# Up projections of a two-layer trunk on one core: three couples of groups instead of two, and two convolution taps multiplied on ScalarE

## The chip, the cores and the metric

The kernel runs on one core of a Trainium2 chip. The metric is the device time of one execution in microseconds; of several runs the median is given. The engines are TensorE (PE, with its weight load PEld), VectorE (DVE), ScalarE (ACT), GpSimd (POOL) and SyncE (SP); transfers go through queues of SP and of POOL.

## The reference, cut to what matters

Two layers of a token mixer and a gated MLP on 256 tokens of width 2048, all in float32. The change lies in the up projection, the convolution and the gate of the MLP:

```python
def conv_ffn(x, w_up, conv_w, conv_b, w_down):
    h = x @ w_up                       # (256, 2048) @ (2048, 11008)
    C = h.shape[-1]
    h = lax.conv_general_dilated(h, conv_w[:, None, :], window_strides=(1,),
                                 padding=[(CONV_W - 1, 0)],
                                 dimension_numbers=('NWC', 'WIO', 'NWC'),
                                 feature_group_count=C) + conv_b
    a, g = jnp.split(h, 2, axis=-1)
    return (jax.nn.silu(g) * a) @ w_down
```

The convolution is causal with three taps: a channel's value at token t is the sum of three tokens t, t-1, t-2, each times a constant of the channel.

## The kernel before, in words

**Products.** Each float32 operand is split into a rounded high part and the low rest, and a product is built of high x high, high x low and low x high. A weight chunk is 128 x 2048 values. It is loaded by SP's queue (`_load`, L105 and L109, three raw rooms), cast to `wh` by ScalarE (L134), and the rest `wl` is subtracted by VectorE (L137). All matmuls stand in line L242.

**Groups.** An up projection has 22 groups, numbered 0 to 21, of four chunks (the last one has two); group 0 is computed at the boundary ahead of it. A group yields two blocks of 128 channels of `a` and two of `g`. There are two ways to compute groups:

- `plain(gi, turned)`: channels on the partitions, tokens along the row. `prod_a` makes 64 matmuls of 512 columns (with `wh`) and 64 of 256 (with `wl`). One accumulator then has two halves of 256 tokens, which `sum_halves` (L409 copy on ScalarE, L411 addition on VectorE) adds.
- `summed(gis)`, a couple: two groups at once, tokens on the partitions. It takes eight chunks in the order `UP_PAIRS`; four are treated as *wide* with 24 matmuls of 512 columns (`eight`), four as *seven* (`UP_SEVEN`) with 21, in the manner of Strassen's seven products. A *seven* chunk needs sums of weights (`ts`, L144) and five rooms (`ts`, `wh`, `wl`, `th`, `tl`), and a combined sum of inputs (`combine`, rooms `xu`). Its banks are named q3, p2, e, q4, p1, q5, p7, p6. At the end, `rest` (L474 to L478) and four additions (L1119) give the values, and the plain group that follows turns them back: 16 transposes into `upr` (L1049), and behind its chunks 1 and 2 it calls `both`, which works through the four pairs of the couple.

**Pair.** `pair` convolves a block of `a` and its block of `g` (`conv`: ScalarE scales by the third tap and adds the bias, L1023; VectorE adds the other taps with two scalar_tensor_tensor, L1024 and L1026), then silu on ScalarE (L1040) and the product on VectorE (L1041). A plain group ends with its two pairs, so their instructions stand in the queues of ScalarE and VectorE among the first splits of what follows.

**Order of the work.** `UP` lists groups and couples: before, 5+6 and 8+9. `EARLY` puts side work behind chunk c of group gi: `restore` (the row's layer norm gets its scale and offset: two rows of constants loaded, four operations on VectorE, L741 and L742), `combine` (one of the four combined sums, L1074 and L314 to L326) and `park` (a store of the residual on POOL's queue). `jobs` is `park_all`: for chunks of the down projection it loads, splits and stores parts ahead of time, one step for each call of `next(jobs)`. Its loads and stores are on POOL's queue.

**Rooms.** The ring `big` has 14 rooms of 128 x 2048 and holds split weights, the combined sums and most activations; `side` has 6. Small tiles of 256 columns are in ring `t1` (T1 rooms), of 512 in `t2` (T2 rooms).

The Tile scheduler orders the instructions of an engine. Each engine runs its queue in that order, so a waiting instruction holds back all that stand behind it.

Of the kernel before, what the change touches and what calls it, by code (L numbers as in the profile page):

```python
# [56 lines left out]
T1, T2 = 6, 5  # L57
# [15 lines left out]
UP = [(1,), (2,), (3,), (4,), (5, 6), (7,), (8, 9), *((i,) for i in range(10, 22))]  # L73
UP_PAIRS = [0, 2, 1, 3, 5, 4, 6, 7]
UP_SEVEN = (2, 3, 4, 6)
EARLY = {(1, 2): ("restore", 0), (2, 1): ("combine", 0), (2, 2): ("restore", 1), (2, 3): ("park", 0),
         (3, 1): ("restore", 2), (3, 2): ("combine", 1), (3, 3): ("restore", 3), (4, 0): ("park", 1),
         (4, 1): ("combine", 2), (4, 2): ("combine", 3)}
# [143 lines left out]
def trunk(ctx: ExitStack, tc: tile.TileContext, x, xT, gm_in, gm_wout, ffn_up, ffn_dn,  # L222
# [12 lines left out]
    def slot(shape, name, dt=F32, tag="big"):  # L235
        return big.tile(shape, dt, tag=tag, name=name, bufs=SLOTS[tag])
# [169 lines left out]

    def sum_halves(acc, name):
        lo = tp.tile([P, S], F32, tag="t1", name=f"lo_{name}", bufs=T1)
        nc.scalar.copy(lo, acc[:, S : 2 * S])  # L409
        h = tp.tile([P, S], F32, tag="t1", name=f"h_{name}", bufs=T1)  # L410
        nc.vector.tensor_tensor(h, acc[:, 0:S], lo, ALU.add)  # L411
        return h
# [605 lines left out]
    def conv(layer, F, acc, name):  # L1018

        h = acc if acc.shape[-1] == S else sum_halves(acc, name)  # L1020
        w = C_CONV + (layer * 2 * NF_FF + F) * 4
        c = tp.tile([P, S], F32, tag="t1", name=f"c_{name}", bufs=T1)
        nc.scalar.activation(c, h, AF.Identity, bias=cst[:, w + 3 : w + 4], scale=cst[:, w + 2 : w + 3])  # L1023
        nc.vector.scalar_tensor_tensor(c[:, 1:S], h[:, 0 : S - 1], cst[:, w + 1 : w + 2], c[:, 1:S],  # L1024
                                       ALU.mult, ALU.add)
        nc.vector.scalar_tensor_tensor(c[:, 2:S], h[:, 0 : S - 2], cst[:, w : w + 1], c[:, 2:S],  # L1026
                                       ALU.mult, ALU.add)
        return c

    def ffn(layer, ln, acc, end, last):  # L1030
# [3 lines left out]
        def pair(a, acc_a, acc_g):  # L1034
            if act[a // 8] is None:
                act[a // 8] = slot([P, 8, S], f"act{layer}_{a // 8}", tag="side" if a // 8 in (0, 5) else "big")
            ca = conv(layer, a, acc_a, f"{layer}a{a}")
            cg = conv(layer, NF_FF + a, acc_g, f"{layer}g{a}")
# [31 lines left out]
        def combine_up(p):  # L1070
# [4 lines left out]
            if len(sums) % 2 == 0:  # L1075
                rooms.append(slot([P, 2, 8 * P], f"xu{layer}_{p}", F32R))
# [4 lines left out]
        def plain(gi, turned):  # L1081
# [3 lines left out]
            for c in range(KD // nk):  # L1085
# [7 lines left out]
                if (gi > 9 and c > 0) or (gi, c) == (7, 3):  # L1093
                    next(jobs, None)
# [466 lines left out]
```

## Time and profile before

| | us |
|---|---|
| median of 3 runs | 2451.52 (2451.03 to 2452.03) |
| the profiled execution | 2450.69 |
| its span in the profile | 2448.9 |
| busy: PE / PEld | 2441.2 / 2066.0 |
| busy: DVE / ACT / POOL | 2187.1 / 1510.8 / 140.2 |

Busy times are those of one profiled execution; the span is the time from its first to its last record. Matmuls are pipelined, so TensorE can be busy without a gap and still be slower than at its peak. Up stages are at 817 to 1264 us (first layer) and 1772 to 2219 us (second layer). L with a number is a line of the kernel before; names such as `wh178` carry the chunk's number, and the profile leaves numbers out. An up_ with a letter is a bank of a couple, `up` an accumulator of a plain group.

### The profile page before, as it was taken

How to read it: one execution, taken by the hardware profiler on the slowest of the kernel's cores; microseconds unless marked ns; L12 is line 12 of the kernel's file. 1: busy time of each engine (PE TensorE's matmuls, PEld its weight loads, DVE VectorE, ACT ScalarE, POOL GpSimd, SP SyncE). 2: the span in 40 equal slices, each digit the busy share in tenths (PEclk: the TensorE clock that was granted, in tenths of full speed). 3: DMA queues.
4: the chain of work that ended last, by engine and by line, in shares of the span. 5: the costliest groups of instructions: out<-in, count | busy, mean ns of one | idle time of the engine just before them, and what ended most of it. 6: DMA issues, size and time to landing. Idle time of an engine off the chain costs nothing.

```text
span 2448.9 us, 32246 instructions
## 1 busy us (share of the span) xinstructions
PE 2441.2 (100%) x12154; PEld 2066.0 (84%) x12154; DVE 2187.1 (89%) x2909; ACT 1510.8 (62%) x1995; POOL 140.2 (6%) x261
## 2 busy tenths in 40 slices
PE   9999999999999999999999999999999999999999
PEld 7888888888888888888888888988888888888887
DVE  7999999889998889998889897878798998888998
ACT  6666665566576655666665566665665666666553
POOL 0000000001010000011000000000000001010000
PEclk9999999999999999999999999999999999999999
DMA  7555666658796655799988885543575589898894
GB/s 293 204 206 206 232 202 206 206 172 302 256 296 241 239 203 194 260 356 377 338 322 320 317 299 170 189 143 126 205 275 180 179 337 363 321 368 304 313 353 178
DMA packets 128763, 627.37 MB, mean 256 GB/s; under 512 B 11592, under 2 KB 15184, under 8 KB 91616
## 3 DMA queue, kind: packets, MB, share of 16 engines
q1 hardware_dynamic: 94224, 462.47, 53.1%
q0 software_dynamic: 34384, 162.86, 17.8%
q8 instruction: 95, 1.56, 0.2%
q14 instruction: 60, 0.49, 0.1%
HBM read 552.35 MB, written 72.93 MB: 255 GB/s over the span
## 4 chain that ended last, share of the span: by engine, by line
PE 95%; DVE 2%; issue 1%; DMA 1%; ACT 1%; SPq 0%; ACTq 0%; DVEq 0%
PE up L242 29%; PE ub L242 16%; PE dn_q L242 8%; PE dn_p L242 6%; PE v_q L242 5%; PE v_p L242 4%; PE up_q L242 2%; PE wo_q L242 2%; PE dn_e L242 2%; PE up_p L242 2%; PE wo_p L242 2%; PE upf L242 2%; PE mo L242 2%; PE v_e L242 2%; PE mkv L242 1%
## 5 line engine op out<-in xcount | busy, mean ns | idle before, releaser
L137 DVE TENSOR_TENSOR wl<-raw,wh 128x1024 fp32r<-128x1024 f32 (+5 forms) x611 | 937.7, 1553 | 106.3 <-ACT wh L134 76.3
L134 ACT CAST wh<-raw 128x1024 fp32r<-128x1024 f32 (+5 forms) x611 | 791.2, 1318 | 312.9 <-PE up L242 72.0
L242 PE MATMUL up<-xhl,wh 128*128 128x512 f32 x2112 | 492.9, 390 | 0.0
L242 PEld LDWEIGHTS up<-xhl,wh 128*128 128x128 f32 x2112 | 392.3, 188 | 78.6
L134 ACT CAST th<-ts 128x1536 fp32r<-128x1536 f32 x194 | 201.5, 1052 | 164.2 <-DVE ts L144 136.9
L242 PEld LDWEIGHTS up<-xhl,wl 128*128 128x128 f32 x2112 | 262.4, 192 | 5.1
L242 PE MATMUL up<-xhl,wl 128*128 128x256 f32 x2112 | 265.1, 283 | 0.0
L137 DVE TENSOR_TENSOR tl<-ts,th 128x1536 fp32r<-128x1536 f32 x194 | 229.6, 1223 | 9.1 <-ACT th L134 4.7
L242 PE MATMUL ub<-wh,xhl 128*128 128x512 f32 x564 | 175.7, 393 | 0.0
L144 DVE TENSOR_TENSOR ts<-ts,raw 128x512 f32<-128x512 f32 x194 | 133.9, 690 | 2.0
L242 PEld LDWEIGHTS ub<-wh,xhl 128*128 128x128 f32 x564 | 105.9, 188 | 23.7 <-issue 1.9
L144 DVE TENSOR_TENSOR ts<-raw 128x1024 f32<-128x1024 f32 x97 | 118.5, 1222 | 2.7 <-DMA raw<-in_gm_in_dram 1.0
L242 PE MATMUL ub<-wl,xhl 128*128 128x512 f32 x282 | 109.8, 389 | 0.0
L242 PE MATMUL v_q<-wh,xhl 128*128 128x512 f32 x224 | 70.7, 391 | 0.1
L242 PEld LDWEIGHTS ub<-wl,xhl 128*128 128x128 f32 x282 | 53.0, 188 | 11.1
L242 PE MATMUL v_p<-wh,xhl 128*128 128x512 f32 x192 | 59.9, 389 | 0.0
L242 PEld LDWEIGHTS v_q<-wh,xhl 128*128 128x128 f32 x224 | 42.1, 188 | 9.7 <-ACT wh L134 1.0
L832 ACT ACTIVATE lny<-lnt,lncol 128x128 f32<-128x128 f32 x96 | 36.5, 469 | 15.7 <-PE lnt L828 15.6
L161 DVE TENSOR_TENSOR praw<-praw 128x512 f32<-128x512 f32 x64 | 44.1, 690 | 0.5
L242 PE MATMUL v_q<-wl,xhl 128*128 128x512 f32 x112 | 43.6, 389 | 0.0
L242 PE MATMUL mo<-wh,oT 128*128 128x512 f32 x128 | 42.7, 411 | 0.0
L242 PEld LDWEIGHTS v_p<-wh,xhl 128*128 128x128 f32 x192 | 36.1, 188 | 7.5
(2073 smaller groups left out, 4820.9 us busy)
## 6 DMA issues: line engine op xcount, KB each, us to landing
raw<-in_ffn_up_dram SPq DMA_DIRECT2D x172, 1024.0 KB, 5.7
raw<-in_gm_in_dram SPq DMA_DIRECT2D x93, 1024.0 KB, 5.2
raw<-in_ffn_dn_dram SPq DMA_DIRECT2D x68, 1024.0 KB, 7.9
raw<-in_gm_wout_dram SPq DMA_DIRECT2D x48, 1024.0 KB, 6.5
praw<-in_ffn_dn_dram POOLq DMA_DIRECT2D x16, 1024.0 KB, 12.8
keptth<-pth POOLq DMA_DIRECT2D x16, 1024.0 KB, 8.5
kepttl<-ptl POOLq DMA_DIRECT2D x16, 1024.0 KB, 8.8
fth<-keptth POOLq DMA_DIRECT2D x16, 1024.0 KB, 9.6
```

What stands on the lines that cost most here:

```text
L134: cast = self.nc.scalar.copy(hi, raw)
L137: self.nc.vector.tensor_tensor(lo, raw, hi.bitcast(F32), ALU.subtract)
L144: add = lambda o, a, b: self.nc.vector.tensor_tensor(o, a, b, ALU.add)
L161: add = lambda o, a, b: pin(nc.vector.tensor_tensor(o, a, b, ALU.add))
L242: recent[0] = nc.tensor.matmul(o, l, r, start=start, stop=stop, skip_group_check=True)
L832: nc.scalar.activation(y[:, j], t[:, j * P : (j + 1) * P], AF.Identity, bias=lncol[:, o : o + 1], scale=lncol[:, g : g + 1])
```

## The change

- `UP` has three couples, 3+4, 6+7 and 9+10. In the first layer couple 9+10 holds chunks 180 to 187.
- `conv_both` replaces `sum_halves` and `conv` for pairs of plain groups: `a` and `g` share tiles of 2 x 256. ScalarE multiplies taps 2 and 3 as well, with `nc.scalar.mul`, four per pair, and VectorE adds both products with one addition per tap over both halves. `conv` stays for the pairs that come from the transposes.
- `EARLY`: all four combines, two restores and one park are in groups 1 and 2; the restores 2 and 3 and the second park are in groups 12, 16 and 17.
- The rooms of combined sums are taken from `side` instead of `big`.
- Parking starts at (8, 3) and is called behind every chunk of groups 13 to 15, in groups 11, 12 and 16 to 21 behind chunks 1 to 3.
- `T1`, `T2` are 5 and 6 instead of 6 and 5.

```diff
-T1, T2 = 6, 5
+T1, T2 = 5, 6
...
-UP = [(1,), (2,), (3,), (4,), (5, 6), (7,), (8, 9), *((i,) for i in range(10, 22))]
+UP = [(1,), (2,), (3, 4), (5,), (6, 7), (8,), (9, 10), *((i,) for i in range(11, 22))]
...
-EARLY = {(1, 2): ("restore", 0), (2, 1): ("combine", 0), (2, 2): ("restore", 1), (2, 3): ("park", 0),
-         (3, 1): ("restore", 2), (3, 2): ("combine", 1), (3, 3): ("restore", 3), (4, 0): ("park", 1),
-         (4, 1): ("combine", 2), (4, 2): ("combine", 3)}
+EARLY = {(1, 1): ("restore", 0), (1, 2): ("combine", 0), (1, 3): ("combine", 1), (2, 0): ("restore", 1),
+         (2, 1): ("combine", 2), (2, 2): ("park", 0), (2, 3): ("combine", 3),
+         (12, 0): ("restore", 2), (16, 0): ("restore", 3), (17, 0): ("park", 1)}
...
-        h = acc if acc.shape[-1] == S else sum_halves(acc, name)
+        h = acc
...
+    def conv_both(layer, a, *accs):
+
+        two = lambda n, dt=F32: tp.tile([P, 2, S], dt, tag="t2", name=f"{n}_{layer}_{a}", bufs=T2)
+        at = [C_CONV + (layer * 2 * NF_FF + F) * 4 for F in (a, NF_FF + a)]
+        lo, c, d, h = two("lo"), two("c"), two("d"), []
+        for i, acc in enumerate(accs):
+            nc.scalar.copy(lo[:, i], acc[:, S : 2 * S])
+            h.append(tp.tile([P, S], F32, tag="t1", name=f"h_{layer}_{a}_{i}", bufs=T1))
+            nc.vector.tensor_tensor(h[i], acc[:, 0:S], lo[:, i], ALU.add)
+        for i, w in enumerate(at):
+            nc.scalar.activation(c[:, i], h[i], AF.Identity, bias=cst[:, w + 3 : w + 4], scale=cst[:, w + 2 : w + 3])
+        for j, t in enumerate((d, lo)):
+            for i, w in enumerate(at):
+                nc.scalar.mul(t[:, i, 1 + j : S], h[i][:, 0 : S - 1 - j], cst[:, w + 1 - j : w + 2 - j])
+            nc.vector.tensor_tensor(c[:, :, 1 + j : S], c[:, :, 1 + j : S], t[:, :, 1 + j : S], ALU.add)
+        return c[:, 0], c[:, 1]
...
-            ca = conv(layer, a, acc_a, f"{layer}a{a}")
-            cg = conv(layer, NF_FF + a, acc_g, f"{layer}g{a}")
+            if acc_a.shape[-1] > S:
+                ca, cg = conv_both(layer, a, acc_a, acc_g)
+            else:
+                ca = conv(layer, a, acc_a, f"{layer}a{a}")
+                cg = conv(layer, NF_FF + a, acc_g, f"{layer}g{a}")
...
-                rooms.append(slot([P, 2, 8 * P], f"xu{layer}_{p}", F32R))
+                rooms.append(slot([P, 2, 8 * P], f"xu{layer}_{p}", F32R, "side"))
...
-                if (gi > 9 and c > 0) or (gi, c) == (7, 3):
+                if (gi > 10 and (c > 0 or 12 < gi < 16)) or (gi, c) == (8, 3):
```

How the entry of a first layer's last couple stands on ScalarE before, at couple 8+9 (chunks 176 to 183; `lo` are copies of the two halves, `c` the scaled blocks of `a` and `g` of pair 14, `s` its silu, and `wh178` the high part of the couple's third chunk):

```order
L409 COPY lo_0a14_7601<-up0_7_0_7369 128x256
L1023 ACTIVATE c_0a14_7605<-h_0a14_7603,cst_176 128x256
L409 COPY lo_0g14_7609<-up0_7_2_7371 128x256
L134 CAST wh178_7647<-raw178_7495 128x2048
L1023 ACTIVATE c_0g14_7613<-h_0g14_7611,cst_176 128x256
L134 CAST wh179_7678<-raw179_7565 128x1536
L1040 ACTIVATE s0_14_7617<-c_0g14_7613 128x256
```

And now, at couple 9+10, where `wh182` is the third chunk's high part (L1036 are the multiplications; the eight rows of pair 16, in the same order, stand just ahead):

```order
L1029 COPY lo_0_17_7762<-up0_8_1_7510 128x256
L1029 COPY lo_0_17_7762<-up0_8_3_7512 128x256
L1053 ACTIVATE s0_16_7759<-c_0_16_7743 128x256
L1033 ACTIVATE c_0_17_7763<-h_0_17_0_7766,cst_176 128x256
L1033 ACTIVATE c_0_17_7763<-h_0_17_1_7769,cst_176 128x256
L1036 ACTIVATE d_0_17_7764<-h_0_17_0_7766,cst_176 128x255
L1036 ACTIVATE d_0_17_7764<-h_0_17_1_7769,cst_176 128x255
L1036 ACTIVATE lo_0_17_7762<-h_0_17_0_7766,cst_176 128x254
L1036 ACTIVATE lo_0_17_7762<-h_0_17_1_7769,cst_176 128x254
L134 CAST wh182_7790<-raw182_7635 128x2048
L1053 ACTIVATE s0_17_7779<-c_0_17_7763 128x256
```

The cast of the couple's third chunk stood within the first pair of the plain group ahead; now both pairs with their multiplications are ahead of it. In 3+4 and 6+7 the cast of the third chunk still stands ahead of the pairs.

On TensorE, the first matmuls with the third chunk before, at couple 8+9 (`th177` and `tl177` are of the second chunk; x2 are two matmuls in a row):

```order
L242 MATMUL up0_8_q3_7639<-wh178_7647,xhl1_0_5891 128x512 x2
L242 MATMUL up0_8_q3_7639<-wl178_7648,xhl1_0_5891 128x512
L242 MATMUL up0_8_q3_7639<-wh178_7647,xhl1_0_5891 128x512 x2
L242 MATMUL up0_8_q3_7639<-wl178_7648,xhl1_0_5891 128x512
L242 MATMUL up0_8_p2_7640<-wh178_7647,xhl1_0_5891 128x512 x2
L242 MATMUL up0_8_p2_7640<-wl178_7648,xhl1_0_5891 128x512
L242 MATMUL up0_8_p7_7645<-th177_7554,xu0_2_6488 128x512 x2
L242 MATMUL up0_8_p7_7645<-tl177_7555,xu0_2_6488 128x512
```

And now, at couple 9+10:

```order
L242 MATMUL up0_9_p6_7789<-tl181_7695,xu0_2_6326 128x512
L242 MATMUL up0_9_q3_7782<-wh182_7790,xhl1_0_5891 128x512 x2
L242 MATMUL up0_9_p2_7783<-wh182_7790,xhl1_0_5891 128x512 x2
L242 MATMUL up0_9_e_7784<-wh182_7790,xhl1_0_5891 128x512 x2
L242 MATMUL up0_9_q4_7785<-wh182_7790,xhl1_0_5891 128x512 x2
L242 MATMUL up0_9_q3_7782<-wl182_7791,xhl1_0_5891 128x512
```

Before, matmuls with the second chunk's sums stood behind the first ones with the third chunk, and high and low parts took turns. Now all of the second chunk's are done first, and eight matmuls with the high part stand ahead of the first with the low part.

More of the change, by code (lines that the diff above doesn't have):

```diff
@@ L405, in prod_a @@
                         mm(a[:, 0:S], w(lo, j, f), x[:, 0:S], False, last)
[L407 to L412, printed above, removed]
     def split_act(src, name):
```

## The prediction

> **What bounds the kernel now.** I read the page first, then the chain that ended last, the busy time by stretches of the first up stage (817 to 1264 us), the waits around the late couple, and the groups by shape. The page's busy row and its row of the chain by engine:
>
> ```profile
> PE 2441.2 (100%) x12154; PEld 2066.0 (84%) x12154; DVE 2187.1 (89%) x2909; ACT 1510.8 (62%) x1995; POOL 140.2 (6%) x261
> PE 95%; DVE 2%; issue 1%; DMA 1%; ACT 1%; SPq 0%; ACTq 0%; DVEq 0%
> ```
>
> TensorE is busy for 2441.2 of 2448.9 us. So time is gained only where TensorE gets less to do, or where one of its few stalls goes; VectorE, 89% busy, is the engine that could become late.
>
> The chain shows the first layer's up stage (columns: start, length, what):
>
> ```profile
> 900.37 1.36 PE up_q L242 x6
> ...
> 941.17 5.54 PE up L242 x32
> 946.71 1.75 PE upr L1049 x16
> ...
> 965.13 1.36 PE up_q L242 x6
> ...
> 1006.33 5.54 PE up L242 x32
> 1011.88 1.75 PE upr L1049 x16
> 1013.62 250.06 PE up L242 x1440
> ```
>
> The last row is 1440 matmul rows of plain groups without a stop; 128 of them make a group: 250.06 / 1440 x 128 = 22.23 us. A couple runs from its first up_q to the next plain group: 941.17 - 900.37 = 40.80 us for couple 5+6, and 1006.33 - 965.13 = 41.20 us for 8+9. The 180 matmuls are the same, so the second has 0.40 us of stall. A couple also costs 16 transposes in the group behind it, 1.75 us.
>
> The second layer's couple 8+9:
>
> ```profile
> 1855.27 1.36 PE up_q L242 x6
> ...
> 1870.72 1.93 ACT wh L134
> ...
> 1931.43 1.65 PE up_p L242 x6
> ...
> 1961.97 5.54 PE up L242 x32
> ...
> 1969.26 250.06 PE up L242 x1440
> ```
>
> Here 5+6 starts at 1855.27 and the group behind 8+9 at 1961.97, 106.70 us. In the first layer without its stall that would be 1006.33 - 900.37 - 0.40 = 105.56. So this layer has 1.14 us of stall, and both layers 1.54. The chain goes through ScalarE's cast at 1870.72 and comes back to TensorE at 1931.43: the work between belongs to ScalarE, VectorE and transfers. The waits of that stretch (engine and line, waited for: total, times, longest):
>
> ```profile
> ACT wh L134 <- DMA raw<-in_ffn_up_dram: 10.7, 5, 3.9
> PEld up_p L242 <- DVE h_1a L411: 0.9, 1, 0.9
> PE up_p L242 <- DVE h_1a L411: 0.5, 1, 0.5
> ```
>
> TensorE's stall hangs on VectorE's queue, where the convolution of the group before a couple stands among the first splits of the couple.
>
> **TensorE's part, step by step.** One more couple per layer replaces two plain groups: 40.80 + 1.75 = 42.55 us for 2 x 22.23 = 44.46, so -1.91 us, and for two layers **-3.8 us**. This is sure as far as the weights arrive; it is TensorE's own time, with nothing beside it to hide it. Everything else in the change is worth only the stalls that it makes or takes away: 1.54 us are there to be taken.
>
> **VectorE's part.** Columns of a group: names, shapes, count | busy us, mean ns:
>
> ```profile
> L1024 DVE SCALAR_TENSOR_TENSOR c_0a<-h_0a,cst,c_0a 128x255 f32<-128x255 f32 x32 | 15.4, 482 | 7.0 <-ACT c_0a L1023 7.0
> L411 DVE TENSOR_TENSOR h_0a<-up,lo_0a 128x256 f32<-128x256 f32 x32 | 13.5, 421 | 8.6 <-ACT lo_0a L409 8.6
> L742 DVE TENSOR_TENSOR sum<-sum,lnp 128x512 f32<-128x512 f32 x4 | 2.7, 693 | 0.0
> L137 DVE TENSOR_TENSOR wl<-raw,wh 128x2048 fp32r<-128x2048 f32 x10 | 22.9, 2290 | 3.3 <-ACT wh L134 3.2
> ```
>
> A pair of a plain group loses four tap operations of 0.48 us and gets two additions of 2 x 255 and 2 x 254 elements, which the trace doesn't show; the nearest row is the addition of 512, 0.69. So 4 x 0.48 - 2 x 0.69 = 0.54 us less per pair. There are 29 such pairs per layer left, some 16 us less of VectorE in each up stage, and more where four pairs now come from the transposes.
>
> The load by stretches (length, then PE, PEld, DVE, ACT, POOL, clock, DMA share, GB/s):
>
> ```profile
> 839.00:861.00 22.00, 22.00 (x128) 19.46 (x128) 21.00 (x36) 12.88 (x19) 0.55 (x1) 1.00 0.90 293
> 965.10:1006.30 41.20, 41.20 (x182) 33.62 (x181) 38.85 (x44) 24.61 (x27) 0.00 (x0) 1.00 0.55 190
> 1006.30:1028.50 22.20, 22.20 (x138) 19.97 (x137) 22.15 (x36) 15.38 (x22) 1.79 (x3) 1.00 0.70 248
> 1050.70:1073.00 22.30, 22.30 (x130) 19.73 (x129) 20.95 (x30) 12.96 (x18) 1.93 (x4) 1.00 1.01 412
> ```
>
> A couple leaves VectorE 2.35 us of 41.20, and the group behind it almost nothing (22.15 of 22.20). With three couples, each followed by one plain group, VectorE must do couple and group in 42.55 + 22.23 = 64.8 us. By these rows it needs 38.85 + 22.15 = 61.0, less 0.54 for each of the two pairs at the couple's entry: about 60. So VectorE has some 5 us to spare in each such stretch, and does not become the bound. Two of the four restores leave groups 1 to 4 for 12 and 16, where no couple is near; they cost four additions of 0.69 each, inside plain groups. The combines move into groups 1 and 2, which have room: 21.00 of 22.00 with a pair's saving on top.
>
> **ScalarE's part.** It gets four multiplications per pair. Their price is not in the trace. The nearest rows:
>
> ```profile
> L1023 ACT ACTIVATE c_0a<-h_0a,cst 128x256 f32<-128x256 f32 x32 | 19.2, 601 | 16.0 <-DVE h_0a L411 15.8
> L1040 ACT ACTIVATE s<-c_0g 128x256 f32<-128x256 f32 x41 | 17.1, 416 | 21.9 <-DVE c_0g L1026 21.9
> L409 ACT COPY lo_0a<-up 128x256 f32<-128x256 f32 x32 | 11.6, 362 | 23.0 <-PE up L242 23.0
> L134 ACT CAST wh<-raw 128x2048 fp32r<-128x2048 f32 x10 | 19.1, 1912 | 3.3 <-issue 1.4 <-DMA raw<-in_ffn_up_dram 1.2 <-PE up_q L242 0.6
> ```
>
> One with two columns of constants takes 0.60 us, one with none 0.42; the multiplication has one, so I take the middle, 0.51. Eight of them, for the two pairs of a group, are 4.1 us (3.3 to 4.8). By the Trainium skill (ScalarE: Activation LUTs, What ACT_TABLE_LOAD costs), 186 ns plus 0.833 ns per element plus 93 ns for a pointer operand, an estimate is 0.49 us each and 3.9 for eight: the sum would not move. On average ScalarE has the room: 12.88 + 4.1 = 17.0 of 22.00. What counts is the order at a couple's entry, because ScalarE's cast wh and VectorE's subtraction wl of the couple's third chunk stand behind both pairs. Issues follow each other some 0.09 us closer than their lengths:
>
> ```profile
> 1079.72 0.60 ACT L1023 ACTIVATE c_0a<-h_0a,cst 128x256 f32<-128x256 f32 x1
> 1080.22 0.36 ACT L409 COPY lo_0g<-up 128x256 f32<-128x256 f32 x1
> 1080.47 2.01 ACT L134 CAST wh<-raw 128x1024 fp32r<-128x1024 f32 x2
> ```
>
> Entry of 9+10, with T0 the couple's first matmul. A matmul takes 40.80 / 180 = 0.227 us; the first chunk has 24 and the second 21, so the third chunk's wh182 is needed at T0 + 10.2. The order puts eight matmuls with wh182 before the first with wl182, which is needed at T0 + 12.0. ScalarE: the first copy starts 0.64 ahead of T0, as in the row below; two copies 0.54; an addition of VectorE 0.42; two scalings and four multiplications, 2 x 0.51 + 4 x 0.42 = 2.7: T0 + 3.0. Two copies 0.54 and the silu, 0.33, which waits for VectorE's second addition (0.69 each): T0 + 4.4. Six more: T0 + 7.1. The cast wh182, 1.91: T0 + 9.0. Then wl182, 2.29: T0 + 11.3. The margins are **1.2 and 0.7 us**.
>
> ```profile
> 964.49 0.37 ACT L409 COPY lo_0a<-up 128x256 f32<-128x256 f32 x1
> 965.24 2.35 DVE L137 TENSOR_TENSOR tl<-ts,th 128x1536 fp32r<-128x1536 f32 x2
> 967.66 1.92 ACT L134 CAST wh<-raw 128x2048 fp32r<-128x2048 f32 x1 [1.45 <-issue]
> ```
>
> Before, the same cast at couple 8+9 ended at 969.58, that is T0 + 4.5: the entry gets 4.5 us later on ScalarE. At couples 3+4 and 6+7 the cast stands ahead of the pairs in the order, so their entries keep 2 us or more. A margin of 0.7 us is less than the 2.35 us that VectorE's two subtractions at 965.24 take, which stood between an addition and its tap; so I don't count the stall at the last couple as gone. I let each layer keep one of 1.14, the larger of the two seen: 2.28 for 1.54, **+0.7 us**. Its bounds are 0 and the rivals below.
>
> By the page's rule that adding and multiplying belong on VectorE and not ScalarE (the Trainium skill, ScalarE: Activation LUTs, Rules for kernel authors), the change goes the wrong way. The rows agree for one operation (0.69 for 512 elements against about 0.51 for 256), yet neither engine's sum sets the end here; what the rule would make of the time is the slower rival below.
>
> **Transfers and rooms.** Parking moves to groups 13 to 15, up to one piece per group. The stretch 1050.70:1073.00 holds a piece being parked and moves 412 GB/s with TensorE busy throughout, and a couple moves 190. Parking in every group would add up to the same rate as that row, so I cost it at nothing; if that cover goes, ScalarE's cast waits as above, up to 3.9 us once. The rooms for combined sums leave the ring of weights, which then has six for weights in groups 12 to 15 and five in 16 and 17, fewer than now; plain groups run there with wh ahead of TensorE, so also nothing. On SP's queue the two rows of constants of a moved restore now stand among the weight loads of groups 12 and 16:
>
> ```profile
> raw<-in_ffn_up_dram SPq DMA_DIRECT2D x172, 1024.0 KB, 5.7
> ```
>
> A row brings 512 columns where a chunk has 2048, so I put it at a quarter of 5.7, 1.4 us, and two at 2.9. A plain group's chunk lasts 22.23 / 4 = 5.56 us and three are in flight, which covers it; bare, it would be 2.9 at each restore. Park 1's store goes from the front of POOL's queue to group 17, behind the parked pieces; nobody reads it before the down stage, so nothing.
>
> **Sum.** -3.8 + 0.7 = -3.1 us. The profiled execution took 2450.69 us, its span is 2448.9; so about 2447.6 and 2445.8. On the median of 2451.52 that gives 2448.4; the profiled one lies 0.8 under it. A measurement of this kernel tells about 0.2%, 4.9 us, from no change, so this is "the same" by that bound.
>
> **Rivals.**
> *All stalls go.* VectorE's relief is enough, margins hold: -3.8 - 1.5 = -5.3, 2446.2 us. For it: VectorE's spare time. Against: the margins of 0.7. Chance 0.13.
> *The stall grows from couple to couple.* It was none at the first couple and 0.40 and 1.14 at the second. If it runs 0, x, 2x, with x as before, a layer has 3x: 3 x 1.54 = 4.6 in both. Then -3.8 - 1.5 + 4.6 = -0.7, 2450.8 us. For it: two of the three couples have just one plain group to recover in. Against: VectorE's 5 us to spare. A wait for transfers of 3.9 once in a layer would come near the same. Chance 0.16.
> *Slower: ScalarE's queue becomes late.* If silu and casts wait behind VectorE's subtractions, the eight multiplications lie open at the entries of 6+7 and 9+10: 4.1 less a margin of 1.0 is 3.1 us, at two couples in two layers 12.4. Then 2451.5 - 5.3 + 12.4 = 2458.6 us. It decides from 5.3 + 4.9 = 10.2 us of stalls, 2.6 at each of the four. For it: ScalarE's 4.5 us later cast. Against: it waited 1.45 us for nothing shown ahead of that cast, so it wasn't pressed. Chance 0.09.
> My forecast has the rest, 0.62.
>
> **How the numbers follow.** The time is 2448.4, the likeliest case's. The range 2445.7 to 2452.7 reaches from all stalls gone to the growing stall with the high price of the multiplications (0.09 more for each of eight is 0.7, at one couple in each layer 1.4), and 0.5 us beyond both, by which the runs shown differ from their median; it leaves out the slower rival. Faster by over 0.2% is below 2446.6: the first rival and 0.02 of the forecast, 0.15. Slower is 0.09. The same: 0.76.
>
> **What would show it.** In the changed profile: TensorE's busy time down by 3.8 us; couples of 40.8 us with at most 1.2 more at the third; multiplications of 0.42 to 0.60 us; additions near 0.69; wh182 done near T0 + 9, with the rows of waits naming VectorE or ScalarE at its matmuls. Wrong would be: couples over 42 us, up groups 13 to 15 waiting for raw transfers, or a stall at 3+4.

## The result and the profile after

| | before | changed |
|---|---|---|
| median, us | 2451.13 (2451.03 to 2452.03, 6 runs) | 2471.45 (2469.43 to 2473.31, 6 runs) |
| ratio, 95% interval | | 1.0083 (1.0073 to 1.0093) |
| profiled execution / its span, us | 2450.69 / 2448.9 | 2469.84 / 2468.1 |

The changed kernel is 20.3 us slower; 2448.4 was forecast, and the range ended at 2452.7. The page of the changed kernel, busy time and chain by engine:

```profile
PE 2444.8 (99%) x12034; PEld 2061.7 (84%) x12034; DVE 2201.8 (89%) x2817; ACT 1601.4 (65%) x2213; POOL 140.6 (6%) x261
PE 86%; DVE 5%; DMA 4%; ACT 3%; issue 1%; SPq 0%; DVEq 0%; ACTq 0%
```

TensorE's share of the chain fell from 95 to 86%: there are stalls now, and the chain leaves TensorE for VectorE, transfers and ScalarE. Where TensorE waited (all of the execution; waited for: total, times, longest):

```profile
PE up L242 <- ACT wh L134: 12.8, 4, 3.6
PE up L242 <- DVE wl L137: 2.1, 3, 0.8
PE up_p L242 <- DVE h L1031: 1.2, 2, 0.8
```

The first two rows are `up`, plain groups, and 14.9 us together. The couples, `up_p`, wait 1.2. I took the start of each group from TensorE's rows and subtracted what a group takes without a stall (22.23, and 40.80 for a couple). What is over, in us:

| layer | 3+4 | 6+7 | 9+10 | 13 | 14 | 15 | 17 |
|---|---|---|---|---|---|---|---|
| first | 0.64 | 0.29 | 0 | 4.74 | 1.02 | 0 | 4.45 |
| second | 1.18 | 0 | 0 | 4.82 | 0.90 | 0.38 | 6.54 |

The couples lost 2.1 us; groups 13 to 17 lost 22.9. The stages lie at 806 to 1273 us and 1769 to 2238.

The third couple itself went as worked out. TensorE's first matmul of 9+10 and of the group behind, from the chain, then ScalarE's and VectorE's rows of the entry:

```profile
986.72 1.36 PE up_q L242 x6
...
1027.52 5.54 PE up L242 x32
```

```profile
986.07 0.83 ACT L1029 COPY lo<-up 128x256 f32<-128x256 f32 x2 [1.17 <-PE up L242]
987.37 1.09 ACT L1033 ACTIVATE c<-h,cst 128x256 f32<-128x256 f32 x2 [0.47 <-DVE h L1031]
988.37 0.89 ACT L1036 ACTIVATE d<-h,cst 128x255 f32<-128x255 f32 x2
...
993.75 1.89 ACT L134 CAST wh<-raw 128x2048 fp32r<-128x2048 f32 x1
```

```profile
995.67 2.29 DVE L137 TENSOR_TENSOR wl<-raw,wh 128x2048 fp32r<-128x2048 f32 x1 [1.11 <-ACT wh L134]
```

T0 is 986.72. wh182 ends at 995.64, T0 + 8.9 (9.0 was worked out); wl182 at 997.96, T0 + 11.2 (11.3). The couple takes 1027.52 - 986.72 = 40.80 us, without a stall: the margins held.

The 22.9 us begin with a restore. Rows around the end of group 12 in the first layer, first SP's queue, then VectorE, ScalarE and TensorE (idle time before, and what ended it, in brackets):

```profile
1061.23 1.89 SPq L731 DMA_DIRECT2D lnp<-in_ln_rows_dram  x2
```

```profile
1070.56 0.69 DVE L734 TENSOR_TENSOR sum<-sum,lnp 128x512 f32<-128x512 f32 x1 [1.49 <-DMA lnp<-in_ln_rows_dram]
...
1074.94 0.69 DVE L735 TENSOR_TENSOR sum<-sum,lnp 128x512 f32<-128x512 f32 x1 [3.35 <-DMA lnp<-in_ln_rows_dram]
...
1079.62 0.42 DVE L1031 TENSOR_TENSOR h<-up,lo 128x256 f32<-128x256 f32 x1
```

```profile
1073.07 0.83 ACT L1029 COPY lo<-up 128x256 f32<-128x256 f32 x2 [3.54 <-PE up L242]
1080.08 0.60 ACT L1033 ACTIVATE c<-h,cst 128x256 f32<-128x256 f32 x1 [6.19 <-DVE h L1031]
...
1086.85 1.03 ACT L134 CAST wh<-raw 128x1024 fp32r<-128x1024 f32 x1
```

```profile
1087.93 5.26 PE L242 MATMUL up<-xhl,wh 128*128 128x512 f32 x16 [3.11 <-ACT wh L134]
```

The two rows of constants are issued at 1061.23 and land as late as 1074.9. VectorE stands in its queue for 1.49 + 3.35 = 4.8 us, and behind it the h addition of group 12's pairs. ScalarE has copied at 1073.07 and waits 6.19 us for that addition. Only then come both pairs with eight multiplications, 1080.08 to 1086.85, and behind them the cast wh of group 13. TensorE waits 3.11 us. In the second layer VectorE's wait is 5.3 us at the same place.

At group 17, which has about half of the 22.9 us, VectorE's own wait for rows is small: 0.2 us here and 0.8 in the second layer. The shape is the same, ScalarE waits 6.02 us for an h addition. But what makes that addition late is work: ScalarE's casts had stood 4.45 us for weights in transit, and then VectorE has the restore's four operations (2.6 us), four subtractions of weights (4.6) and the rest of a parked chunk ahead of the addition at 1174.14.

```profile
1149.95 2.00 ACT L134 CAST wh<-raw 128x1024 fp32r<-128x1024 f32 x2 [4.45 <-DMA raw<-in_ffn_up_dram]
...
1174.59 1.09 ACT L1033 ACTIVATE c<-h,cst 128x256 f32<-128x256 f32 x2 [6.02 <-DVE h L1031]
```

```profile
1165.34 1.29 DVE L734 TENSOR_TENSOR sum<-sum,lnp 128x512 f32<-128x512 f32 x2 [0.17 <-DMA lnp<-in_ln_rows_dram]
...
1167.93 4.62 DVE L137 TENSOR_TENSOR wl<-raw,wh 128x1024 fp32r<-128x1024 f32 x4
```

Before, the loads of restore 2 were the last two of the three in the next row, issued at 833.0 and 839.8 us. VectorE's first operation with the one came at 850.74 and with the other at 851.94, 18 and 12 us behind and without a wait:

```profile
832.49 7.62 SPq L738 DMA_DIRECT2D lnp<-in_ln_rows_dram  x3
```

```profile
850.74 1.29 DVE L741 TENSOR_TENSOR sum<-sum,lnp 128x512 f32<-128x512 f32 x2
851.94 0.69 DVE L742 TENSOR_TENSOR sum<-sum,lnp 128x512 f32<-128x512 f32 x1
```

### The profile page after: what moved, and what is told of

It reads as the page before. It is cut to its first block, busy times and chain, and to the rows that moved or that the text cites. A ratio compares the mean times of both kernels' runs of the same rounds, so it can differ in the third digit from the quotient of the medians.

```text
span 2468.1 us, 32145 instructions
## 1 busy us (share of the span) xinstructions
PE 2444.8 (99%) x12034; PEld 2061.7 (84%) x12034; DVE 2201.8 (89%) x2817; ACT 1601.4 (65%) x2213; POOL 140.6 (6%) x261
## 4 chain that ended last, share of the span: by engine, by line
PE 86%; DVE 5%; DMA 4%; ACT 3%; issue 1%; SPq 0%; DVEq 0%; ACTq 0%
PE ub L242 16%; PE up L242 15%; PE dn_q L242 8%; PE dn_p L242 7%; PE v_q L242 5%; PE up_q L242 4%; PE v_p L242 4%; PE up_p L242 4%; PE dn_e L242 3%; PE wo_q L242 2%; DMA lnp<-in_ln_rows_dram 2%; DVE wl L137 2%; PE wo_p L242 2%; PE upf L242 2%; DMA raw<-in_ffn_up_dram 2%; PE mo L242 2%
## 5 line engine op out<-in xcount | busy, mean ns | idle before, releaser
L137 DVE TENSOR_TENSOR wl<-raw,wh 128x1024 fp32r<-128x1024 f32 (+4 forms) x595 | 928.7, 1581 | 100.1 <-ACT wh L134 84.2
L134 ACT CAST wh<-raw 128x1024 fp32r<-128x1024 f32 (+4 forms) x595 | 783.3, 1342 | 277.3 <-DMA raw<-in_ffn_up_dram 63.0
L242 PE MATMUL up<-xhl,wh 128*128 128x512 f32 x1856 | 440.8, 394 | 12.8 <-ACT wh L134 12.8
L242 PEld LDWEIGHTS up<-xhl,wh 128*128 128x128 f32 x1856 | 348.4, 190 | 85.0 <-ACT wh L134 14.5
L1033 ACT ACTIVATE c<-h,cst 128x256 f32<-128x256 f32 x116 | 64.9, 596 | 42.7 <-DVE h L1031 42.6
L1037 DVE TENSOR_TENSOR c<-c,d 128x510 f32<-128x510 f32 x58 | 39.8, 687 | 21.9 <-ACT d L1036 21.6
L242 PE MATMUL up_p<-wh,xhl 128*128 128x512 f32 x192 | 59.1, 389 | 0.0
L242 PE MATMUL up_q<-wh,xhl 128*128 128x512 f32 x192 | 59.1, 389 | 0.0
L1031 DVE TENSOR_TENSOR h<-up,lo 128x256 f32<-128x256 f32 x116 | 44.7, 417 | 14.8 <-ACT lo L1029 14.8
L1029 ACT COPY lo<-up 128x256 f32<-128x256 f32 x116 | 37.8, 365 | 25.0 <-PE up L242 24.2
```

The lines of the kernel that those rows point to most:

```text
L134: cast = self.nc.scalar.copy(hi, raw)
L137: self.nc.vector.tensor_tensor(lo, raw, hi.bitcast(F32), ALU.subtract)
L242: recent[0] = nc.tensor.matmul(o, l, r, start=start, stop=stop, skip_group_check=True)
L1029: nc.scalar.copy(lo[:, i], acc[:, S : 2 * S])
L1031: nc.vector.tensor_tensor(h[i], acc[:, 0:S], lo[:, i], ALU.add)
L1033: nc.scalar.activation(c[:, i], h[i], AF.Identity, bias=cst[:, w + 3 : w + 4], scale=cst[:, w + 2 : w + 3])
```

## The experiments

The first theory was: VectorE's wait and the restore's operations delay the casts of groups 13 and 17, because there the casts stand behind both pairs (a row of activations has just taken a room). Rivals: parking behind every chunk; a missing room; the multiplications alone. The kernel before was run beside each batch and had medians of 2450.69 to 2451.32 us. Expectations are quoted as they stood. Stalls by group are taken as in the table above, from one profiled execution each.

**Restores in groups 5 and 8**

```diff
-         (12, 0): ("restore", 2), (16, 0): ("restore", 3), (17, 0): ("park", 1)}
+         (5, 0): ("restore", 2), (8, 0): ("restore", 3), (17, 0): ("park", 1)}
```

> The changed kernel with restores 2 and 3 moved from groups 12 and 16 to groups 5 and 8; park 1 stays in group 17, taps stay on ScalarE. Theory (restore): in groups 12 and 16 VectorE waits in its queue for the restore's rows (waits of 4.8 and 0.2 us in the first layer) and does four additions of 0.69, the h additions of the pairs stand behind, and the casts wh of the next group behind the pairs on ScalarE. So the stalls of groups 13, 14 and 17 (10.2 us in the first layer, 12.6 in the second) go nearly: 22 us less, and perhaps 1 to 3 us more at the couples: 2448 to 2453 us. Rival (parking): the stalls come from one step of parking behind every chunk of groups 13 to 15: no change, 2468 to 2473. Rival (taps): they come from eight multiplications ahead of the casts alone: at most a third goes, over 2463.

Measured: 2461.61 us, ratio 1.0046 (1.0029 to 1.0062). The stalls of 13, 14 and 17 are gone in both layers, as expected; 15 has 1.7 us in the first. But 9+10, whose margin was 0.7 us, now loses 5.2 and 5.1 us: the restore in group 8 delays its entry, without a wait for rows. Half of the 20 us moved from one place to another, so the time is above the expected range.

**With park 1 in group 8 too**: `(8, 2): ("park", 1)` in place of `(17, 0)`.

> As the kernel with restores in groups 5 and 8, and park 1 in group 8 too, so that a room of the ring of weights comes free before group 12. Theory (restore): the room is worth nothing, the same time within 1 us. Rival (rooms): the room missing in groups 12 to 17 makes the stalls at 13 and 17, which follow the rows in which the activations take a room; then this one is faster than the one with park 1 in group 17 by 5 us or more.

Measured: 2459.85 us, 1.0038 (1.0023 to 1.0053), with the same stalls within 0.6 us each. A room that comes free earlier is worth nothing here, where 13 and 17 have no stall in either kernel.

**Parking not behind every chunk**

```diff
-                if (gi > 10 and (c > 0 or 12 < gi < 16)) or (gi, c) == (8, 3):
+                if (gi > 10 and c > 0) or (gi, c) == (8, 3):
```

> The changed kernel, with no parking step behind the first chunk of groups 13 to 15, as elsewhere; restores stay in groups 12 and 16. Theory (restore): VectorE's wait at group 12 stays, since parking runs there as before; the stall at group 13 (4.7 us) stays in both layers, those of 14 and 17 may shrink: 2461 to 2470 us. Rival (parking): the stalls are gone: 2448 to 2453.

Measured: 2463.25 us, 1.0049 (1.0034 to 1.0064). Group 13 keeps its stall, 5.0 and 5.7 us; those of 14 and 17 are gone (0.2 left at 17). Yet VectorE waited even longer for rows:

```profile
DVE sum L734 <- DMA lnp<-in_ln_rows_dram: 12.5, 4, 4.3
DVE sum L735 <- DMA lnp<-in_ln_rows_dram: 5.0, 4, 3.0
```

So a wait at group 16 is harmless when the weights have a lead again (here it is 3.3 us in the first layer, and the changed kernel, with 0.2, stalled), and dense parking is what keeps them from it after the first stall. The kernel gives part back at the down stage, where parking that ends later makes TensorE wait 3.9 us for wl.

**Taps on VectorE**: three couples and all else as changed, with `sum_halves`, the old `conv` for all pairs, and T1, T2 = 6, 5.

> The changed kernel with the old convolution (taps 2 and 3 on VectorE by scalar_tensor_tensor, T1 6 and T2 5), all else as changed. Theory (restore): the wait for the rows stays but ScalarE has eight multiplications (4 us) less ahead of the cast wh of groups 13 and 17; of stalls of 4.5 to 6.5 us each 0.5 to 2.5 are left: 2450 to 2458 us, the couples' entries on VectorE included. Rival (restore alone, without the taps): the stalls stay at 13 and 17: 2467 to 2473.

Measured: 2462.90 us, 1.0051 (1.0036 to 1.0066). Neither theory had this: VectorE doesn't wait for a row any more, and still 7.4 and 7.5 us of stalls are there, strewn over groups 12 to 17. SP's queue shows why VectorE doesn't wait:

```profile
1027.29 0.33 SPq L738 DMA_DIRECT2D lnp<-in_ln_rows_dram  x1
1028.97 0.33 SPq L109 DMA_DIRECT2D raw<-in_ffn_up_dram  x1
1033.30 1.30 SPq L738 DMA_DIRECT2D lnp<-in_ln_rows_dram  x3
```

The scheduler pulled the loads of all four rows forward to 1027 to 1034 us, behind couple 9+10, long before groups 12 and 16; SP's queue waits there 4.3 us for the transposes that free the rooms (`SPq L738 <- PE upr`), with weights queued behind. In the changed kernel the loads stand where `EARLY` has them. The rows take rooms of ring t2, and `conv_both` fills its six rooms with `lo`, `c` and `d` of two pairs; that this keeps the loads from moving is argued from the code, not shown.

**No rows loaded**: in restores 2 and 3 the loads are left out, and VectorE's four operations read resident constants.

```diff
             for j in range(2):
+                if f > 1 and self.idx != 1:
+                    continue
...
+            if f > 1 and self.idx != 1:
+                row = [cst[:, 0:512]] * 2
```

> The changed kernel, but the restores in groups 12 and 16 multiply and add resident constants instead of the layer norm's rows: the four loads of rows are left out, the four additions of 0.69 us stay in their places. Theory (wait): VectorE waited 4.8 and 5.3 us for the rows at group 12 and that is what delays the casts of group 13; its stall of 4.7 us goes to at most 1.5 in both layers, while the stall at 17 (waits of 0.2 and 0.8 only) stays at 3 us or more: 2459 to 2465 us. Rival (place): the additions alone, 2.4 us ahead of the pairs, suffice; the stall at 13 stays over 2.5: 2466 us or more.

Measured: 2451.15 us, 1.0001 (0.9992 to 1.0010). The whole 20 us are gone. The reading has a flaw that I saw later: without a load to wait for, the scheduler also moved the operations, in the first layer to 793 to 808 us. Park 1's store went with them, to 808.6 us. So the wait, the place of the operations and that of the park changed together.

**One part alone: `conv_both` in the kernel before**, with T1 5 and T2 6.

> The kernel before with one part of the change: pairs of plain groups by conv_both, T1 5 and T2 6; two couples, restores in groups 1 to 4 and parking as before. Theory (restore): the multiplications take some 4 us of the 4.2 by which the cast was ahead of TensorE at groups 13 and 17, and nothing else comes on top; stalls of 0 to 1.5 there: 2449 to 2454 us. Rival (taps): eight multiplications ahead of the casts are enough for the stalls of 13 and 17 by themselves: 2460 us or more.

Measured: 2450.83 us, 0.9999 (0.9990 to 1.0008). The multiplications on ScalarE alone cost and bring nothing that can be measured.

**Restores in groups 14 and 18**, park 1 in 19:

```diff
-         (12, 0): ("restore", 2), (16, 0): ("restore", 3), (17, 0): ("park", 1)}
+         (14, 0): ("restore", 2), (18, 0): ("restore", 3), (19, 0): ("park", 1)}
```

> The changed kernel with restores 2 and 3 in groups 14 and 18 instead of 12 and 16, park 1 in group 19; parking behind every chunk of groups 13 to 15 stays. Theory (place): groups 12 and 16 are the only ones whose following group has its cast behind both pairs, since there the activations take a room; a wait of VectorE in 14 or 18 meets 6 us or more by which wh is ahead. Stalls of 13 and 17 go, 0 to 3 us stay at 14 or 15, the couples keep 1 to 2: 2448 to 2453 us. Rival (wait anywhere): a wait of 5 us for rows costs the same in any group under parking: 2460 or more.

Measured: 2480.79 us, 1.0120 (1.0106 to 1.0134). My theory of the place falls: 13 and 17 are free, but 15, 19 and 20 now lose 17.0 us in the first layer and 16.3 in the second.

```profile
DVE sum L734 <- DMA lnp<-in_ln_rows_dram: 8.0, 4, 3.5
DVE sum L735 <- DMA lnp<-in_ln_rows_dram: 4.4, 4, 1.9
PE up L242 <- DVE wl L137: 21.3, 11, 3.7
```

So a late VectorE is paid in these groups too; the operation that TensorE meets late is wl itself. Not all of it is rows, for which VectorE waits 12.4 us in both layers. Ahead of a wl in group 19 it is idle for 7.06 us more, and 7.67 in the second layer. By the trace's semaphores that ends as the store of park 1 lands, 14.3 and 14.9 us behind its issue; the cast needed there ended only 0.9 and 1.5 us earlier. The store frees a room of ring `big`, which the weights take next.

**The same with parking thin**, by the edit to `next(jobs)` above:

> Restores in groups 14 and 18, park 1 in 19, and no parking step behind the first chunk of groups 13 to 15. Theory: all stalls after the couples are gone; what stays is 3.8 us less of TensorE's work and 1 to 2.5 us of stalls at the entries of the couples, where before had 1.5: 2447 to 2449 us, faster than the kernel before. Rival (couples): a third couple costs more at the entries than it saves once VectorE runs without cover: over 2451.

Measured: 2465.20 us, 1.0057 (1.0045 to 1.0070). Only 19 stalls behind the couples, 4.0 and 4.7 us. 14 is harmless now, 18 is not.

**Rows loaded, not read**: the loads stay, the operations read constants (the last two lines of that diff alone).

> As the kernel without the loads, but the four rows are loaded in groups 12 and 16 as in the changed kernel; VectorE reads resident constants instead, so nobody waits for the rows. The restored values differ from the reference's. Theory (wait): the cost is VectorE's wait for the landing, so this is near the kernel without loads, 2450 to 2455 us. Rival (transfer): the rows themselves, 256 KB each in SP's queue ahead of the weights and among the parking, make the weights late: 2462 us or more.

Measured: 2452.84 us, 1.0006 (0.9997 to 1.0016). The transfers themselves cost 1.7 us by the medians, and nothing that the intervals tell apart. As above, the operations and the park had moved.

**Rows loaded ahead** into a room of ring `side`, a group before each restore by the code:

```diff
+         (11, 0): ("rows", (2,)), (12, 0): ("restore", 2), (15, 0): ("rows", (3,)), (16, 0): ("restore", 3), (17, 0): ("park", 1)}
...
+            t = slot([P, 2 * len(fs), 512], f"lnr{self.idx}_{fs[0]}", tag="side")
```

> The changed kernel with the rows of restores 2 and 3 loaded a group or more ahead into a room of the ring of 2048 columns (side); restores, parking and taps stay where they are. Theory (wait): the rows have landed when VectorE comes to the restore, the stalls of 13 and 17 go: 2450 to 2455 us. Rival (transfer, or the room that parking lacks): 2460 us or more.

Measured: 2458.99 us, 1.0032 (1.0020 to 1.0043), between the two expectations. With rooms of their own the first rows were issued at 847.64 us, 200 us ahead of group 12, and the restore was pulled into couple 3+4:

```profile
847.64 1.25 SPq L732 DMA_DIRECT2D lnr<-in_ln_rows_dram  x2
```

No wait of VectorE for rows is left, and no stall at 13. At 17 stalls of 7.2 and 1.7 us stay. In the first layer VectorE stands idle there ahead of a wl:

```profile
1167.23 1.23 DVE L137 TENSOR_TENSOR wl<-raw,wh 128x1024 fp32r<-128x1024 f32 x1 [4.19 <-issue]
```

The profile names nothing that ended it. The semaphore that VectorE's queue waits for there is that of park 1's store, issued at 1156.67 and landed 10.5 us later, at 1167.15. In the second layer the store takes 7.8 us and the idle time is 1.53. TensorE waits 4.43 and 1.43 us, and only behind the longer wait does its granted clock fall, to 0.50 for some 4 us.

**Rows loaded ahead, restores in 12 and 13, parking thin:**

```diff
+         (11, 0): ("rows", (2, 3)), (12, 0): ("restore", 2), (13, 0): ("restore", 3), (14, 0): ("park", 1)}
```

> Rows of both restores loaded in one go ahead of group 12, restores in groups 12 and 13, park 1 in 14, no parking step behind the first chunk of groups 13 to 15. Theory (wait): no stall after the couples; TensorE's 3.8 us less and 1 to 2.5 us of stalls at the couples where before had 1.5: 2447 to 2450 us, faster than the kernel before. Rival: the couples' entries eat the gain: 2451 or more.

Measured: 2454.77 us, 1.0016 (1.0008 to 1.0025). No stall in a plain group, but the restores had been pulled forward, six of the eight operations into couple 3+4, which waits:

```profile
PE up_p L242 <- DVE h L1041: 2.9, 2, 1.8
PE dn_q L242 <- DVE wl L137: 2.2, 2, 1.2
```

**Taps on VectorE, no rows loaded**, by both edits above:

> Three couples with the old convolution on VectorE, and no loads of the rows in groups 12 and 16 (resident constants instead, values differ from the reference's); it stands against the kernel without the loads with taps on ScalarE, 2451.15 us. Theory: with the rows gone the taps on ScalarE are a small gain, since VectorE is then nearly full in groups 12 to 16: 2452 to 2458 us here. Rival (taps are a loss): ScalarE's multiplications make the entries late: 2448 to 2450 here.

Measured: 2448.81 us, 0.9992 (0.9983 to 1.0001). Against 2451.15 with the taps on ScalarE the expectation that ScalarE's taps are a small gain does not hold; the two intervals overlap, so that they are a loss is not settled.

**Late restores alone**, in the kernel before:

```diff
-         (3, 1): ("restore", 2), (3, 2): ("combine", 1), (3, 3): ("restore", 3), (4, 0): ("park", 1),
+         (12, 0): ("restore", 2), (3, 2): ("combine", 1), (16, 0): ("restore", 3), (17, 0): ("park", 1),
```

> The kernel before, two couples and the old taps, with one part of the change: restores 2 and 3 in groups 12 and 16 and park 1 in 17. Theory (wait): VectorE waits some 5 us for the rows there too, and the cast at groups 13 and 17 is ahead by only 4.2 us; 3 to 5 us of stall at 13 in each layer, less at 17 since parking is thin: 2456 to 2462 us. Rival (together): the wait costs only with the multiplications behind it on ScalarE: under 2453.

Measured: 2454.59 us, 1.0015 (1.0006 to 1.0024), between both. As with the taps on VectorE, the scheduler pulled the loads forward (to 1009 to 1014 us), and VectorE waits for no row of restores 2 and 3; SP's queue waits 2.8 us for the transposes of couple 8+9. TensorE's longest wait is 2.1 us for an h addition at 1056 us; that it comes from SP's queue is not shown.

**Taps on VectorE, rows ahead**, parking dense and then thin with restores in 12 and 13:

> Three couples, old taps on VectorE, rows of restores 2 and 3 loaded a group ahead, restores in 12 and 16, parking behind every chunk of groups 13 to 15. Theory: the wait is gone; against the same with taps on ScalarE (2458.99) 2 us or more less; parking leaves 1 to 5 us at groups 15 and 17: 2449 to 2456 us. Rival: without late rows nothing is left of the stalls: under 2449.

Measured: 2450.53 us, 0.9999 (0.9990 to 1.0008). With 3.0 and 1.1 us of stalls in the up stages this is the best that computes everything, and not to be told from the kernel before. Restore 2 had again been pulled forward, to 884 to 914 us in the first layer, so this is not a restore in group 12.

> As the last, with both restores in groups 12 and 13, park 1 in 14, and no parking step behind the first chunk of groups 13 to 15. Theory: parking was the rest; no stalls after the couples, under 1 us at them: 2447 to 2449.5 us, faster than the kernel before. Rival (parking that ends later makes the down stage's start late): 2450 to 2453.

Measured: 2459.31 us, 1.0037 (1.0023 to 1.0051). The down stage's start is late, as the rival had it, and dearer than it said: the up stages have no stall over 0.2 us, but h additions of the last pairs stand in the down stage's way. That later parking is what delays them is not shown.

```profile
PE dn_p L242 <- DVE h_1a L411: 3.5, 2, 3.0
PE dn_p L242 <- DVE h_0a L411: 3.0, 1, 3.0
```

**Rows and restores pinned**, so that the scheduler may not move them: loads in group 11, operations in 12 and 13, park 1 in 14, dense parking; taps on ScalarE, then on VectorE.

```diff
+                    tc.keep_in_program_order(nc.sync.dma_start(t[:, 2 * i + j], src.to_broadcast([P, 512])))
...
+                    done = nc.vector.tensor_tensor(self.r(b, f), self.r(b, f), row[j], op)
+                    if f > 1 and self.idx != 1:
+                        tc.keep_in_program_order(done)
```

> The changed kernel, taps on ScalarE; the four rows of restores 2 and 3 are loaded in group 11 into one room of the ring of 2048 columns, the restores stand in groups 12 and 13 and the scheduler may not move them; park 1 in 14, parking behind every chunk of groups 13 to 15. Theory (wait): as without the loads, 2450 to 2453 us. Rival (rows or additions cost by themselves under parking): over 2456.

Measured: 2459.65 us, 1.0031 (1.0020 to 1.0042). No wait for rows of restores 2 and 3, yet 10.4 us of stalls in the two layers, the largest at group 14 (2.5 and 2.0). So the wait for rows is not all that costs there; the operations are the first suspect.

> The same with the old taps on VectorE. Theory: 2448 to 2450 us, the best of all that load their rows; by the runs before, 2 us less than with the taps on ScalarE. Rival (VectorE full in groups 12 and 13): over 2451.

Measured: 2465.31 us, 1.0055 (1.0041 to 1.0069); stalls at 13 of 3.7 and 4.1 us, further ones to 17. The rival, that VectorE is full there with the old taps, fits; nothing else was varied to show it.

**Operations pinned in 12 and 16, no rows loaded**, to part waits from operations: the diff of the kernel without loads, and the last three lines of the one above.

> The changed kernel with the operations of restores 2 and 3 pinned in groups 12 and 16, on resident constants; the four loads of rows are left out, so the restored values differ from the reference's. Theory (wait): most of the 20 us was the wait for the rows; without it 2453 to 2460 us, no stall over 1.5 at group 13. Rival (operations): the eight operations of 0.69 us among dense parking are enough, 2464 us or more.

Measured: 2455.65 us, 1.0018 (1.0009 to 1.0028). The end of group 12 again:

```profile
1059.11 0.68 DVE L739 TENSOR_TENSOR sum<-sum,cst 128x512 f32<-128x512 f32 x1
...
1064.05 1.28 DVE L739 TENSOR_TENSOR sum<-sum,cst 128x512 f32<-128x512 f32 x2
...
1066.99 0.69 DVE L739 TENSOR_TENSOR sum<-sum,cst 128x512 f32<-128x512 f32 x1
```

```profile
1073.80 0.83 ACT L1035 COPY lo<-up 128x256 f32<-128x256 f32 x2 [4.13 <-PE up L242]
1075.79 0.60 ACT L1039 ACTIVATE c<-h,cst 128x256 f32<-128x256 f32 x1 [1.17 <-DVE h L1037]
...
1082.57 1.04 ACT L134 CAST wh<-raw 128x1024 fp32r<-128x1024 f32 x1
```

VectorE's four operations run with no idle time ahead of them. ScalarE waits 1.17 us for h, not 6.19, and casts at 1082.57, not 1086.85; group 13 has no stall. With nothing to wait for they also come 11 us earlier than in the changed kernel (1059.11, not 1070.56). At 17 stalls of 1.5 and 1.7 us are left.

Of the changed kernel's 20.3 us, 2471.45 - 2455.65 = 15.8 go with the rows: the wait for them, the later place that it gives the operations, and the loads, which unread cost 1.7. The other 2455.65 - 2451.15 = 4.5 are what stays in groups 12 and 16: the operations, and park 1's store behind them. No run parts these two.

## Why the prediction was wrong

- **TensorE's part was right.** -3.8 us was forecast. In the kernel with no rows loaded, the second layer's stage takes 456.0 us with 0.2 of stalls, and before 458.7 with 1.1: 455.8 against 457.6, -1.8 a layer. In the changed kernel the sign that was named for it, TensorE's busy time down by 3.8, is hidden: it rose from 2441.2 to 2444.8, with matmuls at a lower clock behind the stalls (last section). With no rows loaded it is 2438.5, 2.7 down.
- **The multiplications and the couples' entries were right in size.** 0.51 us was taken and 0.50 measured, 0.69 for an addition and 0.69 measured. The couples lost 2.1 us against 2.28. That sum is luck: the place was wrong, it was mostly 3+4, which the forecast had named as a sign of being wrong, and not the last couple.

```profile
L1036 ACT ACTIVATE d<-h,cst 128x255 f32<-128x255 f32 x56 | 25.7, 496 | 0.0
L1037 DVE TENSOR_TENSOR c<-c,d 128x510 f32<-128x510 f32 x28 | 19.2, 687 | 10.3 <-ACT d L1036 10.2
```

- **The step that failed** is the one on the moved restores: "they cost four additions of 0.69 each, inside plain groups", and for their loads "A plain group's chunk lasts 22.23 / 4 = 5.56 us and three are in flight, which covers it". It asked only what the loads do to SP's queue. It never asked who waits for the rows: VectorE, in order, with the h additions, ScalarE's pairs and the next casts behind it. The forecast put the bare cost at 2.9 us a restore as a delay of weights; VectorE's wait was 4.8 and 5.3 us at group 12, and the stall with all that follows 15.8 us. The landing was mis-sized too: a row was put at a quarter of a chunk's 5.7 us, 1.4; the two at group 12 took 9.3 and 13.0 us, and in the kernel before none landed in less than 3.3.
- **Parking, "so I cost it at nothing",** failed in part. It makes no stall by itself: with restores in 5 and 8 and dense parking, 13, 14 and 17 are free. But it takes away the lead that heals one: with thin parking the stalls of 14 and 17 are gone though VectorE waits longer.
- **Park 1, "nobody reads it before the down stage, so nothing",** looked for readers alone. In the changed kernel no idle time of VectorE or ScalarE ends with its landing. But the room that it frees is written next, and with the rows ahead VectorE stood 4.19 us for it. The kernel before shows that wait already, in group 4, where TensorE did not feel it:

```profile
881.34 1.23 DVE L137 TENSOR_TENSOR wl<-raw,wh 128x1024 fp32r<-128x1024 f32 x1 [3.85 <-DMA resd<-sum]
```

- **"On average ScalarE has the room"** was right, and misleading. Alone, the multiplications cost nothing (0.9999). Behind a wait they stand ahead of the next cast: with rows waited for, the taps on ScalarE go with 2471.45 and those on VectorE with 2462.90 us, where the loads had moved too.
- **The slower rival had the right shape and the wrong place.** "ScalarE's queue becomes late" is what happened, with both pairs ahead of a cast; but at groups 13 and 17, and at 13 for a wait that the rival didn't have. By the Trainium skill (ScalarE: Activation LUTs, Rules for kernel authors) a multiplication belongs on VectorE; the run with that part alone shows no difference, so the rule doesn't explain the loss.

What stays open: how the late restore and the dense parking share the stall at 17, which goes when either is changed; and whether a version exists that beats the kernel before; none here did.

## What to carry to other kernels

A small load that is moved is to be priced at its reader: when is it issued, when does it land under the traffic of the new place, and what stands behind the reader on its in-order engine. A moved store that frees a room is to be priced at the next writer of that room. A scheduler decides both times: compare issue and first use in the traces; a load with a room of its own may be pulled far ahead, and its reader with it, to a worse place. An experiment that removes a wait can set its operations free to move as well: look where they went before reading the time.

## What was not expected of the hardware

After three of the changed kernel's four longer stalls TensorE ran slow. The changed kernel's span and mean clock, its wait at group 17 as TensorE's row, and stretches behind the stalls at groups 13 and 17 of the first layer and 13 of the second (length, PE, PEld, DVE, ACT, POOL, granted clock, DMA share, GB/s):

```profile
core 0: 2468.1 us, clock 0.997
```

```profile
1182.05 5.54 PE L242 MATMUL up<-xhl,wh 128*128 128x512 f32 x16 [2.54 <-ACT wh L134]
```

```profile
1080.00:1084.00 4.00, 4.00 (x24) 3.47 (x24) 3.76 (x8) 3.29 (x9) 0.00 (x0) 1.00 0.85 295
1087.90:1091.90 4.00, 3.97 (x12) 3.17 (x13) 3.63 (x4) 4.00 (x5) 0.56 (x1) 0.64 0.31 33
1091.90:1096.00 4.10, 4.10 (x31) 3.88 (x30) 4.10 (x4) 4.10 (x4) 0.53 (x1) 1.00 0.77 228
...
1182.00:1186.00 4.00, 3.95 (x11) 3.14 (x12) 3.97 (x5) 4.00 (x5) 0.00 (x0) 0.62 0.93 357
...
2051.50:2055.50 4.00, 3.94 (x18) 3.28 (x19) 3.58 (x4) 4.00 (x6) 0.56 (x1) 1.00 0.16 20
```

Behind an idle time of 3.11 us the granted clock is 0.64 for 4 us; behind 2.54 us it is 0.62, and behind 3.61 us, at group 17 of the second layer, 0.50. So the first layer's stall at 13 costs 4.74 - 3.11 = 1.6 us more than the wait. It does not follow the length of the wait alone: behind 3.57 us, at group 13 of the second layer, the clock stays at 1.00. The mean clock of the execution, 0.997, is about 0.003 x 2468 = 7 us of the loss, and with the 14.9 us of waits it makes the 22.9 of the groups within 1 us. The Trainium skill (TensorE: Matmul & The Clock Gate, What's actually happening) has an idle TensorE fall back to half clock after an idle window of about 3.4 us; here 3.11 us, and 2.54 at group 17, were enough, and 3.57 once were not.

The rows of 256 KB, broadcast to all partitions, landed late under parking: at group 12 of the first layer 9.3 us behind their issue and 13.0 (issued at 1061.87, VectorE's wait for it over at 1074.9), in the second 11.7 and 12.9. The weights of four times the size took 7.6 us (median) in the same stretch of the first.
